# Second attention: when biases and weights to split are loaded, and where the probabilities are transposed

## The chip, the core and the metric

The kernel runs on one core of a Trainium2 chip. The metric is device time in microseconds (us), as the median of several executions. The core's engines are called PE (matrix products), ACT (scalar engine), DVE (vector engine), POOL (GpSimd) and SP, which here only issues DMA transfers. ACT issues some transfers too. All transfers of the core share 16 DMA engines.

## What is computed

One layer of an encoder, for two requests of 2048 tokens and width 1024, all in fp32:

```
proj = rms_norm(x) @ w_in
o_a  = windowed attention (8 query heads, 2 key heads)   * silu(g_a)
o_b  = neighbourhood attention (8 heads, 64-wide grid)   * silu(g_b)
x    = x + concat(o_a, o_b) @ w_out
y    = x + (p @ w_ple) * sigmoid(x @ w_ple_gate)
```

The neighbourhood attention lets a query of the 32 x 64 grid see 8 rows and 16 columns around it. Scores get a learned bias by relative place, and cells outside the window a bias of -1e30, so that softmax gives them zero:

```
sc = where(mask, einsum('bnqhd,banchd->bnhqac', qr, kb) * scale + bias, -inf)
pr = softmax(sc)
o  = einsum('bnhqac,banchd->bnqhd', pr, vb)
```

## The kernel before, in words

**Precision.** An fp32 product is made of three products of split operands: each operand is written as a high part in the type fp32r and a remainder, and high x high, high x low and low x high are added in PSUM. The split of an operand is a cast on ACT (high) and a subtraction on DVE or POOL (low). Weights that are used often are split once, in `presplit`: a block is loaded into the tile `pre` (L224), split, and stored to DRAM (`sp_...`, L217), from where the split parts are loaded later.

**Units.** The program runs 96 attention units, f = 0 to 95. Units 0 to 31 are the first attention, units 32 to 95 the second one: two halves of four heads, two requests, 16 blocks of 128 queries (4 blocks of rows by 4 of columns, the column block is cb = f mod 4). While the attention of unit f is on PE, the products of the input projection of a later unit (`pqk`, `pvg`: 48 matmuls of 512 columns) fill the room between its small products. A second attention's unit takes some 15 us. After the units comes the output projection.

**A unit of the second attention** (`unit_b`) does, for its four heads: scores on PE (`scb`) and a softmax step on DVE that adds the tile `bias` and takes the row maximum (L286); the exponentials on ACT (L310, tile `s`); transposes of the probabilities on PE (`pt`, tile `ptb`); their split by a cast on ACT and a subtraction on DVE (`p_t`, L946 and L947); the product with the values (`po`, tile `pob`, values in `vw`, loaded at L912); and the gate and the store (`fin`, store `ob_d` at L975).

**Copied and fp32 units.** PE transposes an fp32r tile faster than an fp32 one (medians of 227 and 272 ns a matmul). In most units (`copied_(f)`: 32 to 54 and 59 to 86) the exponentials are copied by DMA into the fp32r tile `tn` before they are transposed. ACT issues these four copies itself, right behind the exponentials:

```
if sink is None and turned is not None:
    waiting.append(i)
    for k in waiting[:1] if n_ in (1, 2) else waiting[:] if n_ == 3 else ():
        P(nc.scalar.dma_start(to.bitcast(F32), ss[k]))   # tn <- s, L319
```

The other units (55 to 58 and 87 to 95, the "fp32 units") transpose the fp32 tile directly (rows `ptb<-rowwise,s`).

**What sets the order.** Three things. A plan per kind of unit says at which share of the unit's PE work each step is put; `PLAN_C` is the one of the copied units, and an entry is (share, this unit or the one before, step, head). PE's order is pinned to it. The other engines' orders are made by a scheduler, which puts an instruction as early as its dependencies let it, unless it is wrapped in `P` (kept in the order in which the program was written) or has an added dependency (`after(load, ex)`: the load waits for that instruction by a semaphore). And a transfer takes one of eight completion counters (DMAHW0 to DMAHW7) in turn, over SP and ACT together; before it is issued, the transfer eight places before it, which had the same counter, has to be complete. An engine's queue is served in order, so whatever stands behind a waiting transfer on SP or ACT waits with it.

**The bias.** Two slots in turn hold the bias of a unit; a unit with cb = 2 uses the one of the unit before it. Its load (L897) must wait until the softmax steps that read the slot's old content are done. For a copied unit behind a copied unit the load also waits for the last exponential of the unit before (`last_ex[-1]`).

Of the kernel before, what the change touches and what calls it, by code (L numbers as in the profile page):

```python
# [11 lines left out]
F32 = mybir.dt.float32  # L12
# [7 lines left out]
NT = SEQ // 128  # L20
# [22 lines left out]
def row_type(b):  # L43
    return (0, 1, 1, 2)[b]


def col_type(cb):
    return (0, 1, 1, 2)[cb]
# [10 lines left out]
def bias_offsets():  # L59
# [44 lines left out]
PLAN_C = (  # L104
    (0.00, 1, "sc", 0), (0.03, 1, "sc", 1), (0.07, 1, "sc", 2), (0.09, 0, "po", 2), (0.11, 1, "sc", 3), (0.16, 0, "po", 3),
    (0.16, 1, "exp", 0), (0.24, 0, "fin", 0), (0.35, 1, "prep", 0),
    (0.60, 1, "pt", 0), (0.70, 1, "pt", 1), (0.80, 1, "pt", 2), (0.92, 1, "po", 0), (0.95, 1, "pt", 3), (0.98, 1, "po", 1),
)


def copied_(f):

    return 2 * NT <= f and not (4 * NT - 9 <= f < 4 * NT - 5 or f >= 6 * NT - 9)


def emit(ctx, tc, io):
    nc = tc.nc
# [56 lines left out]
    P = tc.keep_in_program_order  # L174
# [15 lines left out]
    def w_block(half, tag, j):  # L190

        if half == "p":
            return io["w_ple"][128 * j:128 * j + 128, 512 * tag:512 * tag + 512]
        if half == "o":
            h, c = int(tag[2]) - 1, int(tag[1]) - 1
            return io["w_out"][512 * h + 128 * j:512 * h + 128 * j + 128, 512 * c:512 * c + 512]
        c0 = 1280 + 1024 * half + (512 if tag == "wb" else 0)
        return io["w_in"][128 * j:128 * j + 128, c0:c0 + 512]
# [13 lines left out]
    def presplit(load):  # L212

        if load:
            if due:
                key, t, slot = due.pop()
                nc.sync.dma_start(parts_d[key], t[:, 0:2].bitcast(F32))  # L217
            if to_split and (to_split[0][0] in (0, 1) or combined):
                if not pre:
                    pre.extend([ap.tile([128, 4, 512], F32R, tag="raw", name="pre", bufs=1), 0])  # L220
                pre[1] += 1
                due.append((to_split.pop(0), pre[0], 2 + pre[1] % 2))
                key, t, slot = due[0]
                nc.sync.dma_start(t[:, slot].bitcast(F32), w_block(*key))  # L224
            else:
                pre.clear()
        elif due:
            key, t, slot = due[0]
            raw, sc = t[:, slot].bitcast(F32), nw[:, key[2]:key[2] + 1]
            if key[0] in ("p", "o"):  # L230
                behind(nc.scalar.copy(t[:, 0], raw))
                behind(nc.vector.tensor_tensor(out=t[:, 1], in0=raw, in1=t[:, 0].bitcast(F32), op=ALU.subtract))
            else:
                behind(nc.scalar.activation(t[:, 0], raw, AF.Copy, scale=sc))
                behind(nc.vector.scalar_tensor_tensor(out=t[:, 1], in0=raw, scalar=sc, in1=t[:, 0].bitcast(F32),
                                                      op0=ALU.mult, op1=ALU.subtract))
# [23 lines left out]
    def behind(ins, other=None):  # L260

        tc.add_manual_dep(ins.ins, (other or last_pe[-1]).name,
                          mybir.DependencyInfo(mybir.DependencyClass.NoSync, mybir.DependencyReason.DATA),
                          reason="behind the product")
# [25 lines left out]
    def sm_tiles():  # L290
        return {"s": [], **{k: ap.tile([128, 4], F32, tag=k, name=k, bufs=3) for k in ("mx", "nm", "den", "rd")}}

    last_ex = []

    def after(ins, other):

        tc.add_manual_dep(ins.ins, other.name, mybir.DependencyInfo(mybir.DependencyClass.Sync, mybir.DependencyReason.DATA),
                          reason="behind the copies")
# [111 lines left out]
    def big(shape, dt, name):  # L410
        return ap.tile(shape, dt, tag="big", name=name, bufs=3)
# [81 lines left out]
    for i in range(2):  # L493
        t = ap.tile([128, 2, 512], F32R, tag=f"q2{i}", name=f"q2{i}")
# [24 lines left out]
    def proj_a(f):  # L519
# [84 lines left out]
        for i, c in enumerate(project(pg, xr, lambda k, b: w_g[k][:, b, :], 215)):  # L604
            if i in HG and f > 0 and not early:
                split(f + 1, HG[i], low=nc.vector if f == 1 else nc.gpsimd)
            if i in HN and f > 0 and f not in last:
                square(f + 1, HN[i])
            if i == PR:
                queries()  # L610
            if i in (PA, PA + 16) and 1 < f < 2 * NT - 2:
                presplit(i == PA)
            if i == PA and f == 2 * NT - 2:
                store_last()
            if i == 7 and t == NT - 1:
                ps = ptile([128, 512], "ms", "pms")
                tr(ps[:NT, :128], ms_a[:, NT * s:NT * s + NT])
                row = ap.tile([128, 512], F32, tag="sq", name="row", bufs=2)
                P(nc.scalar.copy(row[:NT, :128], ps[:NT, :128]))
                P(nc.sync.dma_start(ms_d[s * SEQ:(s + 1) * SEQ].rearrange("(t p) -> t p", p=128), row[:NT, :128]))  # L620
            yield c
            if i + 24 == ka:
                keys_a(kt, t)
# [172 lines left out]
    def proj_b(f):  # L796
# [10 lines left out]
        for i, c in enumerate(project(pk, xr, lambda k, b: ready("wa", k, w_qk)[:, b, :], 215)):  # L807
            at = i + 24 if f in last else i
            if i == PD and f == 2 * NT + 9:
                stats_b(1)  # L810
            if at in HX:
                split(f + 1, HX[at])
            if i == PA and f >= 2 * NT + 2 and (to_split or due):
                presplit(True)
            yield c
# [18 lines left out]
        for i, c in enumerate(project(pv, xr, lambda k, b: ready("wb", k, w_vg)[:, b, :], 215)):  # L834
            if i + 24 in HX and f not in last:
                split(f + 1, HX[i + 24])
            if i == (PR if f not in last else 1):
                normed()
            if i == PA + 16:
                presplit(False)  # L840
            yield c
            if i == (KB if f not in last else 10):
                if f < 2 * NT + 2:
                    pending.append((kt, b, cb))
                else:
                    keys_b(kt, b, cb)
# [31 lines left out]
            nc.gpsimd.tensor_copy(q1[e][z:z + 64], q1[e][a:a + 64])  # L878
        return q1, q2

    bt = []

    def unit_b(f):
        half, st = divmod(f - 2 * NT, 2 * NT)
# [2 lines left out]
        _, gs = held[f]  # L887
# [4 lines left out]
        if cb != 2:  # L892
            off, _ = BIAS_OFF[(row_type(b), col_type(cb))]
            if not bt:
                bt.append(big([128, 2, 4, 512], F32, "bias"))
            bt.append(bt[0][:, len(bt) % 2])
            load = nc.sync.dma_start(bt[-1][:, :, :n],  # L897
                                     io["bias"][half][:, off:off + 4 * n].rearrange("p (h n) -> p h n", h=4))
            if f > 2 * NT and copied_(f) and copied_(f - 1):
                after(load, last_ex[-1])  # L900
        bias = bt[-1]
        vw = []

        def load_values():

            spare = f >= 6 * NT - 6 and f % 2 == 0
            if spare:
                four = ap.tile([128, 4, 4, 2 * HD], F32R, tag="raw", name="vw4", bufs=1)
            for j in range(nch):
                v = four[:, j] if spare else \  # L910
                    ap.tile([128, 4, 2 * HD], F32R, tag=("vp", "vr_")[j % 2], name="vw", bufs=3 - j % 2)
                load = nc.sync.dma_start(v[:kn[j]].bitcast(F32).rearrange("p h d -> p (h d)"),  # L912
                                         v_d[half, s, cb][r0 + ch[j][0]:r0 + sum(ch[j])]
                                         .rearrange("r c h a d -> (r c) (h a d)"))
                if copied_(f):
                    after(load, last_ex[2])
                vw.append(v)
# [4 lines left out]
        sm, p_ts, got = sm_tiles(), [], {}  # L922
# [45 lines left out]
        def fin(_):  # L968
            pgt = ptile([128, 2, 128], "sc", "pgtb")
            for i in range(2):  # L970
# [3 lines left out]
            nc.vector.tensor_tensor(out=o_t, in0=pgt, in1=o_t, op=ALU.mult)  # L974
            nc.sync.dma_start(ob_d[s][b, :, 2 * half:2 * half + 2, cb, :], o_t)  # L975
        return {"sc": sc, "pt": pt, "po": po, "fin": fin, "prep": lambda _: nxt(f),
                "exp": lambda _: (next(got["ex"]), load_values())}


    tiles = [(s, u) for s in range(2) for u in range(NU)]  # L980
# [89 lines left out]
    def nxt(f):  # L1070
        if f + 1 < 6 * NT:
            qs[f + 1] = prep_a(f + 1) if f + 1 < 2 * NT else prep_b(f + 1)
# [66 lines left out]
    for f in range(6 * NT):  # L1139
# [8 lines left out]
        for kv in range(2 if in_a else 1):  # L1148
            unit = unit_a(f, kv) if in_a else unit_b(f)
            for part, now, act, i in PLAN_A if in_a else PLAN_C if copied_(f) else PLAN_B:  # L1150
                at = (kv + part) / (2 if in_a else 1)
                while spent < at * total:
                    spent += next(stream, total)
                if now or prev:
                    (unit if now else prev)[act](i)
            prev = unit
# [323 lines left out]
```

## Time and profile before

| What | Value |
|---|---|
| median of 3 runs | 2468.09 us (2463.90, 2468.09, 2469.24) |
| profiled execution: its own time | 2468.76 us |
| profiled execution: span of the profile | 2466.9 us |
| mean granted PE clock | 0.999 of full speed |
| busy: PE / DVE / ACT / POOL | 99% / 69% / 57% / 35% |
| units 32 to 95 on PE | about 800 to 1820 us |
| units 55 to 58 on PE (transposes of `s`) | from 1175 us |
| bytes moved by DMA | 479.65 MB, mean 194 GB/s |

How to read the rows of the trace: a timeline row has the start in us, the duration, the engine, the line, the operation, output<-input, the shape, and in brackets the idle time of the engine just before it and what ended it. `SPq` and `ACTq` rows are issues of transfers, not the transfers. A row of a wait view has the waiting engine, line and what it waited for: us in total, number of times, longest. A row of the stage view has the stretch, its length, the busy time of each engine with its number of instructions, then the granted PE clock, the busy share of the DMA engines and the GB/s that they moved.

### The profile page before, as it was taken

Reading aid. Unit: us, or ns where it says so; the run is one execution under the profiler, and the core shown is the slowest. Engines: PE = TensorE matmul, PEld = TensorE weight load, DVE = VectorE, ACT = ScalarE, POOL = GpSimd, SP = SyncE. Lnnn points to the kernel's source line nnn. Section 1 sums busy time; section 2 is a strip of 40 time slices with the busy share of each in tenths; the row PEclk is TensorE's granted clock in tenths of the full one; section 3 lists DMA queues with packets and bytes.
Section 4 is the critical chain, followed back from the end, with each engine's and each line's share of the span. In section 5 each row is a group of like instructions: output and inputs, shape, how many; then the busy total and the mean of one; then the engine's idle time right before and its main releaser. Section 6 shows DMA issues by size and latency. Waiting matters only on the chain.

```text
span 2466.9 us, 40869 instructions
## 1 busy us (share of the span) xinstructions
PE 2443.6 (99%) x13062; PEld 2065.4 (84%) x13062; DVE 1702.1 (69%) x4214; ACT 1412.6 (57%) x3408; POOL 852.9 (35%) x1363
## 2 busy tenths in 40 slices
PE   9999999999999999999999999999999999999999
PEld 8888888888888888888888888878888888888887
DVE  7777777777765666666666666766537655677776
ACT  6777776777664665665666566665763212344443
POOL 4555555555543544554444444433110000000000
PEclk9999999999999999999999999999999999999999
DMA  6332223232254677767967687778977445856765
GB/s 227 122 103 93 95 88 103 95 101 90 93 180 140 212 243 237 234 211 252 305 222 228 207 266 254 246 241 265 312 237 272 156 166 176 269 178 210 247 226 171
DMA packets 275255, 479.65 MB, mean 194 GB/s; under 512 B 31168, under 2 KB 116064, under 8 KB 270816
## 3 DMA queue, kind: packets, MB, share of 16 engines
q1 hardware_dynamic: 245376, 437.84, 53.4%
q10 hardware_dynamic: 29664, 39.19, 5.2%
q8 instruction: 104, 1.70, 0.3%
q14 instruction: 111, 0.91, 0.1%
HBM read 307.72 MB, written 134.23 MB: 179 GB/s over the span
## 4 chain that ended last, share of the span: by engine, by line
PE 90%; DMA 4%; DVE 3%; ACT 2%; issue 1%; POOL 1%; SPq 0%; ACTq 0%; DVEq 0%; POOLq 0%
PE acca L1283 14%; PE pvg L267 14%; PE pqk L267 13%; PE accc L1283 11%; PE pq L267 6%; PE pg L267 6%; PE scb L267 4%; PE pob L267 3%; PE pk L267 3%; PE pple L267 3%; PE po L267 3%; PE sc L267 3%; PE pt L273 2%; DMA vw<-v_d 2%; PE ptb L271 2%; DMA tn<-s 1%
## 5 line engine op out<-in xcount | busy, mean ns | idle before, releaser
L267 PE MATMUL pvg<-wb,xr 128*128 128x512 f32 x1536 | 448.5, 404 | 0.0
L267 PE MATMUL pqk<-wa,xr 128*128 128x512 f32 x1536 | 444.1, 411 | 0.0
L310 ACT ACTIVATE s<-s,nm 128x320 f32<-128x320 f32 (+6 forms) x512 | 293.2, 574 | 150.4 <-DVE nm L307 118.9
L267 PEld LDWEIGHTS pvg<-wb,xr 128*128 128x128 f32 x1536 | 270.4, 189 | 33.5
L267 PEld LDWEIGHTS pqk<-wa,xr 128*128 128x128 f32 x1536 | 266.9, 189 | 37.5
L1265 ACT CAST opd<-raw 128x512 fp32r<-128x512 f32 x224 | 131.5, 619 | 270.3 <-PE acca L1283 118.0
L388 POOL TENSOR_TENSOR xr<-stx,xr 128x512 fp32r<-128x512 f32 x186 | 237.5, 1294 | 116.1 <-ACT xr L387 88.1
L1266 DVE TENSOR_TENSOR opd<-raw,opd 128x512 fp32r<-128x512 f32 x224 | 146.6, 686 | 146.6 <-ACT opd L1265 146.6
L267 PE MATMUL pg<-wb,xr 128*128 128x512 f32 x768 | 232.8, 409 | 1.0 <-DVE vv L545 1.0
L267 PE MATMUL pq<-wa,xr 128*128 128x512 f32 x768 | 219.4, 400 | 0.0
L947 DVE TENSOR_TENSOR p_t<-ptb,p_t 128x368 fp32r<-128x368 f32 (+5 forms) x256 | 120.6, 486 | 100.1 <-ACT p_t L946 97.9
L1283 PE MATMUL accc<-opd,wb 128*128 128x512 f32 x768 | 176.7, 389 | 0.0
L1283 PE MATMUL acca<-opd,wa 128*128 128x512 f32 (+1 forms) x780 | 175.9, 386 | 0.5 <-ACT r L1361 0.5
L1283 PE MATMUL acca<-opd,s 128*128 128x512 f32 x768 | 175.4, 389 | 0.0
L1283 PEld LDWEIGHTS acca<-opd,wa 128*128 128x128 f32 x780 | 144.9, 188 | 30.2 <-ACT r L1361 0.7
L1283 PEld LDWEIGHTS acca<-opd,s 128*128 128x128 f32 x768 | 144.1, 188 | 29.9
L1283 PEld LDWEIGHTS accc<-opd,wb 128*128 128x128 f32 x768 | 144.1, 188 | 29.9
L965 ACT COPY otb<-pob 64x512 f32<-64x512 f32 x128 | 74.4, 582 | 160.7 <-PE pob L267 158.9
L946 ACT CAST p_t<-ptb 128x368 fp32r<-128x368 f32 (+5 forms) x256 | 107.2, 425 | 101.7 <-PE ptb L271 59.8
L152 POOL TENSOR_TENSOR yb<-vrb,power 128x8 f32<-128x8 f32 x64 | 106.5, 1665 | 148.6 <-DVE vrb L822 124.2
L267 PEld LDWEIGHTS pob<-p_t,vw 128*128 128x128 f32 (+2 forms) x832 | 133.7, 189 | 28.2 <-DMA vw<-v_d 6.5
L267 PEld LDWEIGHTS pq<-wa,xr 128*128 128x128 f32 x768 | 135.1, 189 | 17.3
(173 smaller groups left out, 5191.5 us busy)
## 6 DMA issues: line engine op xcount, KB each, us to landing
stx<-x_b SPq DMA_DIRECT2D x128, 256.0 KB
vw<-v_d SPq DMA_DIRECT2D x96, 256.0 KB
stx<-x_a SPq DMA_DIRECT2D x64, 256.0 KB
stn<-x_n SPq DMA_DIRECT2D x64, 256.0 KB
v_d<-vb SPq DMA_DIRECT2D x64, 256.0 KB
ple_d<-ev SPq DMA_DIRECT2D x64, 256.0 KB
xres<-x_r SPq DMA_DIRECT2D x64, 256.0 KB
x_d<-r SPq DMA_DIRECT2D x64, 256.0 KB
```

Source lines behind the costliest of these rows:

```text
L152: nc.gpsimd.tensor_tensor(out=y, in0=v, in1=power.broadcast_to([128, n]), op=ALU.pow)
L267: pinned(nc.tensor.matmul(out, lhsT, rhs, start=start, stop=stop))
L271: pinned(nc.tensor.transpose(out.bitcast(F32R), in_, eye))
L273: pinned(nc.tensor.transpose(out, in_, eye.bitcast(F32)))
L310: ex = nc.scalar.activation(ss[i], ss[i], AF.Exp, bias=nm[:, i:i + 1], accum_out=den[:, i:i + 1])
L388: low.tensor_tensor(out=lo, in0=raw, in1=hi.bitcast(F32), op=ALU.subtract)
L946: nc.scalar.copy(hi, pf)
L947: nc.vector.tensor_tensor(out=lo, in0=pf, in1=hi.bitcast(F32), op=ALU.subtract)
L965: nc.scalar.copy(ot[a:a + 64], pq[z:z + 64])
L1265: P(nc.scalar.copy(hi, v))
L1266: P(nc.vector.tensor_tensor(out=lo, in0=v, in1=hi.bitcast(F32), op=ALU.subtract))
L1283: pinned(nc.tensor.matmul(ps[:, cols], w[k][:, a, c:c + 128], o[:, b, cols], start=i in (0, 1, 4) and k == 0 and j == 0, stop=k == 3 and j ...
```

## The change

Three edits; the arithmetic, the instructions and the bytes moved are the same.

```
 PLAN_C = (
     ... (0.16, 1, "exp", 0), (0.24, 0, "fin", 0), (0.35, 1, "prep", 0),
-    (0.60, 1, "pt", 0), (0.70, 1, "pt", 1), (0.80, 1, "pt", 2), (0.92, 1, "po", 0), (0.95, 1, "pt", 3), (0.98, 1, "po", 1),
+    (0.64, 1, "pt", 0), (0.73, 1, "pt", 1), (0.82, 1, "pt", 2), (0.93, 1, "po", 0), (0.96, 1, "pt", 3), (0.99, 1, "po", 1),
 )
@@ presplit
-                nc.sync.dma_start(t[:, slot].bitcast(F32), w_block(*key))
+                (P if key[0] in ("p", "o") else lambda ins: ins)(nc.sync.dma_start(t[:, slot].bitcast(F32), w_block(*key)))
@@ unit_b
-    bt = []
+    bt, ex_of = [], {}
...
-            if f > 2 * NT and copied_(f) and copied_(f - 1):
-                after(load, last_ex[-1])
+            k = f - (1 if copied_(f) else 3)
+            if copied_(k):
+                after(load, ex_of[k])
...
-                "exp": lambda _: (next(got["ex"]), load_values())}
+                "exp": lambda _: (next(got["ex"]), ex_of.update({f: last_ex[-1]}), load_values())}
```

The first edit moves the transposes of a copied unit later by 0.01 to 0.04 of the unit. The second keeps the 16 loads of `w_ple` and `w_out` blocks to be split in program order on SP. The third is the same as before for copied units; the bias load of an fp32 unit f now waits for the last exponential of unit f - 3, where that is a copied unit (f = 55, 56, 57, 87, 88, 89). Line numbers behind L899 grow by one.

**Place 1: SP in units 52 and 53, and ACT's copies there.** The 360-wide bias row with the DVE wait is that of fp32 unit 55, the 480-wide one that of unit 53 (`stx`: tokens of a later unit; names `v_d`: values of all units, in DRAM). Before:

```order
L370 DMA stx<-x_b 128x512 [waits DMAHW1_49,Pool_49]
L897 DMA bias<-bias 128x4x360 [waits DMAHW2_49,DVE_49]
L975 DMA ob_d_86<-o_tb 128x2x128 [waits DMAHW4_49,DVE_49]
L912 DMA vw<-v_d_302 120x512 [waits DMAHW6_49,PE_49,Activation_49]
L912 DMA vw<-v_d_302 120x512 [waits DMAHW7_49]
L912 DMA vw<-v_d_302 120x512 [waits DMAHW3_49,DMAHW1_49,PE_49]
L897 DMA bias<-bias 128x4x480 [waits DMAHW3_49,Activation_49]
```

After, from unit 53's bias on:

```order
L897 DMA bias<-bias 128x4x480 [waits DMAHW2_49,Activation_49]
L855 DMA v_d_303<-vb 8x8x512 [waits DMAHW3_49,DVE_49]
L855 DMA v_d_304<-vb 16x8x512 [waits DMAHW4_49]
L855 DMA v_d_305<-vb 8x8x512 [waits DMAHW5_49]
L370 DMA stx<-x_b 128x512 [waits DMAHW6_49,Pool_49]
L370 DMA stx<-x_b 128x512 [waits DMAHW7_49,DMAHW1_49,Pool_49]
L897 DMA bias<-bias 128x4x360 [waits DMAHW0_49]
L976 DMA ob_d_86<-o_tb 128x2x128 [waits DMAHW2_49,DVE_49]
```

Unit 55's bias stood in unit 52's stretch of the queue, ahead of unit 53's own; now it stands in unit 53's stretch, and no longer waits for DVE. The copies on ACT, unit 52 before (360 wide):

```order
L319 DMA tn<-s 128x360 [waits DMAHW3_49,DMAHW2_49,Activation_49]
L310 ACTIVATE s,den<-s,nm 128x360
L319 DMA tn<-s 128x360 [waits DMAHW5_49,Activation_49]
L310 ACTIVATE s,den<-s,nm 128x360 [waits DMAHW6_49]
L319 DMA tn<-s 128x360 [waits DMAHW0_49,Activation_49]
L319 DMA tn<-s 128x360 [waits DMAHW2_49,Activation_49]
L875 ACTIVATE q1b<-pqtb,wk 64x256 [waits PE_49]
```

and unit 53 after (480 wide):

```order
L319 DMA tn<-s 128x480 [waits DMAHW3_49,Activation_49]
L310 ACTIVATE s,den<-s,nm 128x480 [waits DMAHW7_49]
L319 DMA tn<-s 128x480 [waits DMAHW6_49,Activation_49]
L319 DMA tn<-s 128x480 [waits DMAHW0_49,Activation_49]
L875 ACTIVATE q1b<-pqtb,wk 64x256 [waits PE_49]
```

In unit 52 the fourth copy had the counter DMAHW2 behind unit 55's bias; now that fourth copy follows an `stx` load, and it is the fourth copy of unit 53 that has the counter of unit 55's bias, DMAHW0. Units 84 and 85, with unit 87's bias, stand to each other in the same way.

**Place 2: SP in units 69 and 70.** `pre<-w_ple` is a block to split. Before:

```order
L655 DMA sums_237<-raw 128x2048
L370 DMA stx<-x_b 128x512 x2
L224 DMA pre<-w_ple 128x512 x2
L975 DMA ob_d_85<-o_tb 128x2x128
L912 DMA vw<-v_d_307 128x512 x2
L912 DMA vw<-v_d_307 96x512
L912 DMA vw<-v_d_307 128x512
L855 DMA v_d_308<-vb 8x8x512
L855 DMA v_d_309<-vb 16x8x512
L370 DMA stx<-x_b 128x512 x2
```

After:

```order
L655 DMA sums_237<-raw 128x2048
L370 DMA stx<-x_b 128x512 x2
L976 DMA ob_d_85<-o_tb 128x2x128
L913 DMA vw<-v_d_307 128x512 x2
L913 DMA vw<-v_d_307 96x512
L913 DMA vw<-v_d_307 128x512
L855 DMA v_d_308<-vb 8x8x512
L855 DMA v_d_309<-vb 16x8x512
L224 DMA pre<-w_ple 128x512
L370 DMA stx<-x_b 128x512 x2
```

The pair of loads in unit 69 is gone; one stands in unit 70, ahead of the two `stx` loads, and from there on each of these loads stands ahead of `stx` instead of behind it.

**Place 3: PE, the transposes of a copied unit**, as one piece of the difference:

```order
 L267 MATMUL pqk<-wa_9495,xr 128x512 x3
-L267 MATMUL pqk<-wa_9497,xr 128x512 x2
+L267 MATMUL pqk<-wa_9497,xr 128x512 x3
+L267 MATMUL pqk<-wa_9499,xr 128x512
 L271 MATMUL ptb<-rowwise,tn 96x128 x3
-L267 MATMUL pqk<-wa_9497,xr 128x512
-L267 MATMUL pqk<-wa_9499,xr 128x512 x3
-L267 MATMUL pqk<-wa_9501,xr 128x512
+L267 MATMUL pqk<-wa_9499,xr 128x512 x2
+L267 MATMUL pqk<-wa_9501,xr 128x512 x3
 L271 MATMUL ptb<-rowwise,tn 96x128 x3
```

The first two heads' transposes stand two of the 24 `pqk` matmuls later; the third and fourth, further down, one later; the `pob` products keep their places.

## The prediction

> **What bounds the kernel now.** I read the page's first part, then who waited for whom on PE.
>
> ```profile
> span 2466.9 us, 40869 instructions
> PE 2443.6 (99%) x13062; PEld 2065.4 (84%) x13062; DVE 1702.1 (69%) x4214; ACT 1412.6 (57%) x3408; POOL 852.9 (35%) x1363
> ...
> PE ptb L271 <- DMA tn<-s: 6.8, 4, 2.9
> PE pob L267 <- DMA vw<-v_d: 3.3, 8, 1.1
> PE scb L267 <- DVE mx L286: 2.1, 1, 2.1
> ```
>
> PE is the bound, and the change leaves its instructions alone. So it can win only PE's idle time, 2466.9 - 2443.6 = 23.3 us in all, or what that idle time does to the clock. The largest item is transposes that wait for copied probabilities: 6.8 us, and only four times. The timelines of PE, ACT and of the issues on SP and ACT show where (in each group: bias or weights issued, the unit's first copy issued, the end of ACT's wait, PE's).
>
> ```profile
> 1119.17 0.38 SPq L897 DMA_DIRECT2D bias<-bias  x1
> 1120.68 0.47 ACTq L319 DMA_DIRECT2D tn<-s  x1
> 1126.63 0.47 ACT L875 ACTIVATE q1b<-pqtb,wk 64x256 fp32r<-64x256 f32 x1 [4.09 <-DMA bias<-bias]
> 1126.78 0.44 PE L271 MATMUL ptb<-rowwise,tn 128*120 128x128 f32 x3 [1.87 <-DMA tn<-s]
> ...
> 1394.72 0.81 SPq L224 DMA_DIRECT2D pre<-w_ple  x2
> 1399.65 0.47 ACT L875 ACTIVATE q1b<-pqtb,wk 64x256 fp32r<-64x256 f32 x1 [2.43 <-DMA pre<-w_ple]
> 1401.23 0.53 PE L271 MATMUL ptb<-rowwise,tn 128*128 128x128 f32 x4 [1.91 <-DMA tn<-s]
> ...
> 1636.49 0.38 SPq L897 DMA_DIRECT2D bias<-bias  x1
> 1638.00 0.47 ACTq L319 DMA_DIRECT2D tn<-s  x1
> 1644.76 0.47 ACT L875 ACTIVATE q1b<-pqtb,wk 64x256 fp32r<-64x256 f32 x1 [4.90 <-DMA bias<-bias]
> 1645.10 0.56 PE L271 MATMUL ptb<-rowwise,tn 128*120 128x128 f32 x3 [2.88 <-DMA tn<-s]
> ```
>
> These are units 52, 69 and 84, the three in which a large load that belongs to a later unit is issued 1.5 us or less ahead of the copies (1120.68 - 1119.17 = 1.51; 1638.00 - 1636.49 = 1.51). Two things follow. The copies share the DMA engines with that load and land late, so the first transposes wait. And ACT, whose fourth copy has the load's completion counter, is held until the load is complete. All three loads are the ones that the change moves.
>
> The stretches around the stalls show a second price, in the clock (the column before the last two):
>
> ```profile
> 1125.00:1130.00 5.00, 3.22 (x20) 2.68 (x21) 2.71 (x5) 3.32 (x9) 1.62 (x3) 1.00 0.96 255
> 1400.00:1405.00 5.00, 3.77 (x17) 3.20 (x18) 4.05 (x8) 3.13 (x8) 0.79 (x2) 0.79 0.98 315
> 1405.00:1410.00 5.00, 5.00 (x30) 4.26 (x29) 1.18 (x3) 2.68 (x6) 2.54 (x2) 0.87 0.13 36
> 1645.00:1650.00 5.00, 4.90 (x20) 3.97 (x21) 4.21 (x9) 4.45 (x11) 1.45 (x3) 0.66 0.82 256
> ```
>
> Behind two of the three stalls the granted clock falls: 5 x (0.21 + 0.13) = 1.70 us lost behind 1401, 5 x 0.34 = 1.70 behind 1645, none behind 1126. What it cost PE is seen from a unit's first transpose to its last product, against an undisturbed unit of the same shape:
>
> ```profile
> 1409.07 0.57 PE L267 MATMUL pob<-p_t,vw 128*128 128x256 f32 x4
> 1662.72 0.45 PE L271 MATMUL ptb<-rowwise,tn 128*128 128x128 f32 x4
> 1669.02 0.57 PE L267 MATMUL pob<-p_t,vw 128*128 128x256 f32 x4
> 1132.82 0.47 PE L267 MATMUL pob<-p_t,vw 120*128 120x256 f32 x3
> 1652.52 0.47 PE L267 MATMUL pob<-p_t,vw 120*128 120x256 f32 x3
> ```
>
> Unit 69: 1409.07 - 1401.23 = 7.84 us, against 1669.02 - 1662.72 = 6.30: 1.54 more. Unit 84: 1652.52 - 1645.10 = 7.42, against 1132.82 - 1126.78 = 6.04: 1.38 more. So the dips cost 2.9 us (3.4 by the clock column).
>
> **The bias loads (third edit).** For copied units the wait is the old one. Unit 55's and unit 87's loads leave the stretches of units 52 and 84 and go one unit on, behind the `stx` loads there:
>
> ```profile
> 1131.84 1.60 SPq L370 DMA_DIRECT2D stx<-x_b  x2
> 1139.07 0.47 ACTq L319 DMA_DIRECT2D tn<-s  x1
> ...
> 1650.77 1.83 SPq L370 DMA_DIRECT2D stx<-x_b  x2
> 1658.77 0.47 ACTq L319 DMA_DIRECT2D tn<-s  x1
> ...
> 1135.00:1140.00 5.00, 5.00 (x29) 4.19 (x27) 4.00 (x12) 2.33 (x6) 2.40 (x2) 1.00 0.11 40
> 1655.00:1660.00 5.00, 5.00 (x29) 4.17 (x28) 3.87 (x11) 2.63 (x7) 2.24 (x2) 1.00 0.05 21
> ```
>
> The exponential of three units back is long done by then, so the new wait itself holds nothing; its effect is the place. The load is issued at about 1133.4 and 1652.6 on the old time scale, 5.6 and 6.2 us ahead of the unit's first copy instead of 1.5, thus over 4 us more lead. With the old landing time the stall would be at most 2.88 - 4.1, below nothing. The bytes fit too: behind those places the DMA engines stood at 0.11 and 0.05 of 5 us, and 720 KB at the 256 GB/s of the row at 1645 are 2.8 us. ACT's fourth copy there has the bias's counter. It is issued some 2 us behind the first, so 7.7 and 8.2 us behind the load. In units 52 and 84 ACT was free again at 1126.6 and 1644.8, 7.5 and 8.3 us behind the load, so ACT may wait a few tenths. PE does not see that: `q1b` serves the next unit. Bounds: both stalls fully gone, -4.75; or both reappear in units 53 and 85, 0. I take -4.75. Queued behind the load on SP is `ob_d`, which waits for DVE some 5.8 us anyway (295.3 / 51 in the row below).
>
> **The loads to split (second edit).** The pair of unit 69 goes, so 512 KB leave the place ahead of its copies. Its late issue has a row too (the second; the first is that of `ob_d`):
>
> ```profile
> SPq L975 <- DVE o_tb L974: 295.3, 51, 8.5
> ...
> SPq L224 <- DMA sums<-raw: 4.9, 1, 4.9
> ```
>
> SP stood 4.9 us in front of the pair for the completion of `sums`. That counter now belongs to the unit's third copy, which comes behind 1394.72, when `sums` was complete. From unit 70 on each load (256 KB, about 1 us at 256 GB/s) stands ahead of two `stx` loads instead of behind them. `stx` feeds a split a unit later, so 1 us more is covered; without that cover it would be 1 us in 15 units. The splits of `pre` stay at their places on ACT and DVE, 40 projection matmuls behind the load's place. Bounds: -1.91 or 0; I take -1.91.
>
> **The transposes (first edit).** The first two heads' transposes come two matmuls later:
>
> ```profile
> 1127.05 1.40 PE L267 MATMUL pqk<-wa,xr 128*128 128x512 f32 x5
> 1128.29 0.36 PE L271 MATMUL ptb<-rowwise,tn 128*120 128x128 f32 x3
> ```
>
> Five `pqk` matmuls take 1.24 us, two 0.5 us: so much more time for the copies. That covers the fourth and smallest stall, unit 86's 0.17 us (6.83 is the sum of the four), whose bias is not moved. The matmuls only change places, so the move itself costs PE nothing. What comes nearer is the last head's transpose to the next unit's third score product, which takes over its PSUM bank (three banks in turn):
>
> ```profile
> 1132.96 0.46 DVE L947 TENSOR_TENSOR p_t<-ptb,p_t 120x288 fp32r<-120x288 f32 x1 [1.21 <-ACT p_t L946]
> 1134.97 0.39 PE L267 MATMUL scb<-ks_b,q1b 128*128 128x480 f32 x1
> ```
>
> DVE is done with the bank at 1133.42, the product comes at 1134.97: 1.55 us of room, of which one matmul takes 0.25. No cost. The `pob` products keep their places and the `vw` loads theirs, so I leave the 3.3 us there (bounds: none, or twice as much).
>
> **Sum.** 1.87 + 2.88 + 1.91 + 0.17 = 6.83 us of stalls and 2.9 us of dips make 9.7. The profiled execution took 2468.76 us, so 2459.0; the median, 2468.09, is 0.67 below it, so **2458.4 us**. Behind the stalls PE is bound everywhere, so what is won there reaches the end.
>
> The Trainium skill, TensorE: Matmul & The Clock Gate, Part 1 and its closing table, says that the clock falls to half after an idle window of some 3.4 us, and to avoid PE gaps over about 3 us. The size agrees (1.70 us is half of 3.4); the cause does not: rows 1401 and 1645 dip behind 1.91 and 2.88 us. By the Trainium skill these gaps would be harmless to the clock; what would then follow is rival 1.
>
> **Rivals.**
> 1. The dips are not owed to these stalls (the gap of 1.87 us has none, and one of 2.1 us in the list above stays) and come elsewhere, or the median's executions had fewer of them: only 6.8 us are won, 2461.3. For it: one stall in three without a dip. Against: in the stage view of the whole span in steps of 20 us only the two stretches with these two stalls are below 1.00.
> 2. The stalls move with the loads: units 53 and 85 wait for the bias, a unit behind 69 for its weights. Unit 86 has this very order now:
>
> ```profile
> 1673.98 0.38 SPq L897 DMA_DIRECT2D bias<-bias  x1
> 1675.59 0.47 ACTq L319 DMA_DIRECT2D tn<-s  x1
> 1679.88 0.53 PE L271 MATMUL ptb<-rowwise,tn 128*128 128x128 f32 x4 [0.17 <-DMA tn<-s]
> ```
>
> There even 1.6 us of lead cost only 0.17. If two of three stalls came back, 2 to 3 us with their clock would be won: 2465.5.
> 3. Slower: the bank of the last transpose. If DVE reaches it 1.3 us later than now, the third score product waits in every copied unit, 51 of them. From that point on each 0.2 us costs 51 x 0.2 = 10 us: 2458.4 + 20 = 2478 at 0.4. Against it: 1.3 us is three of DVE's steps of that kind, and DVE waited 1.21 us for work just ahead.
>
> **How the numbers follow.** Forecast 0.60, rival 1 0.20, rival 2 0.14, rival 3 0.06. A run of three rounds can tell about 0.2% from no change, 4.9 us, so below 2463.2 is faster. That gives faster 0.80 (forecast and rival 1), same 0.14, slower 0.06. The forecast's own range is 2456.0 (some `vw` waits go with the loads) to 2460.5. The range reaches over rival 1 and most of rival 2: 2455.5 to 2465.5.
>
> **What would show it.** Right: no PE wait of `ptb` for `tn` over 0.5 us; no ACT wait for `bias` in units 52 and 84 nor for `pre` in 69; clock 1.00 in all stretches from 800 to 1820; PE busy unchanged but for the dips, and some 13 us idle left. Wrong: waits of `ptb` in units 53, 85 or 70 to 72, or a new wait of `scb` for DVE in many units. The forecast falls if the dips remain without the stalls.

## The result, and the profile after

The changed kernel took 2463.16 us (median of 20 executions, 2458.59 to 2466.03), the kernel before beside it 2468.16 us (median of 20, 2463.14 to 2473.02). The ratio is 0.9983, with a 95% interval of 0.9976 to 0.9990. So the change wins 5.0 us by the medians and 4.3 by the means; 9.7 were forecast. The gain is surely there. Against the line that the prediction drew for "faster" it can't be placed: by the medians (2463.16 against 2463.2) it lies just past that line, by the ratio (0.17% against 0.2%) just short of it.

The page of the changed kernel, the span and the row of busy times:

```profile
span 2459.8 us, 40879 instructions
PE 2442.1 (99%) x13062; PEld 2065.0 (84%) x13062; DVE 1701.3 (69%) x4214; ACT 1407.7 (57%) x3408; POOL 850.7 (35%) x1363
```

The view of who waited for whom, its two largest rows on PE and the one of the bias on ACT (us in total, times, longest):

```profile
PE scb L267 <- DVE mx L286: 3.2, 1, 3.2
PE pob L267 <- DMA vw<-v_d: 3.0, 6, 0.6
...
ACT q1b L875 <- DMA bias<-bias: 1.7, 1, 1.7
```

and the row of the kernel before that answers to the last one:

```profile
ACT q1b L875 <- DMA bias<-bias: 11.3, 3, 4.9
```

PE's idle time is 2459.8 - 2442.1 = 17.7 us, against 23.3. No row `ptb <- DMA tn` is left: all four stalls of 6.8 us are gone. ACT's 11.3 us behind `bias` are down to 1.7 us, one wait, in unit 86, whose load was not moved; ACT's row for `pre` is gone too. The profiled execution took 2461.64 us, 7.1 less than that of before. But the stall of the score product in unit 92, 2.11 us before, is 3.16 now, and the clock dips behind it. The timelines of ACT, DVE and PE there, in the changed kernel:

```profile
1757.76 0.58 ACT L1062 COPY ev<-pple 128x512 f32<-128x512 f32 x1 [4.06 <-DMA ple_d<-ev]
1759.02 0.69 DVE L1001 TENSOR_TENSOR p_r<-p,p_r 128x512 fp32r<-128x512 f32 x1 [4.60 <-ACT p_r L1000]
1760.14 0.61 PE L267 MATMUL scb<-ks_b,q1b 128*128 128x288 f32 x1 [3.16 <-DVE mx L286]
```

and its stages (length, PE's busy time and instructions, granted clock, DMA share, GB/s):

```profile
1735.00:1740.00 5.00, 5.00 (x33) 1.00 1.05 357
1740.00:1745.00 5.00, 5.00 (x30) 1.00 1.06 398
1745.00:1750.00 5.00, 5.00 (x31) 1.00 1.06 402
...
1755.00:1760.00 5.00, 1.98 (x12) 0.91 0.99 377
1760.00:1765.00 5.00, 4.86 (x15) 0.50 0.69 184
1765.00:1770.00 5.00, 5.00 (x29) 0.91 0.96 304
```

From 1735 on the DMA engines are full. A store of the per-layer path (`ple_d<-ev`) completes late, and ACT is held for 4.06 us at the next evacuation into that buffer. The cast of `p_r` behind it comes late. DVE, whose next step is the subtraction that goes with this cast, stands idle for 4.60 us, does its softmax step only behind that, and PE waits 3.16 us for it. The clock loses 5 x (0.09 + 0.50 + 0.09) = 3.4 us. In the profile of before the same place had 2.11 us and no dip. That is the first candidate for the missing half.

The second candidate is the profile of before itself: the sum was made from one execution.

### The profile page after: what moved, and what is told of

Same layout as the page of the kernel before. It is cut to its first block, busy times and chain, and to the rows that moved or that the text cites. A ratio compares the mean times of both kernels' runs of the same rounds, so it can differ in the third digit from the quotient of the medians.

```text
span 2459.8 us, 40879 instructions
## 1 busy us (share of the span) xinstructions
PE 2442.1 (99%) x13062; PEld 2065.0 (84%) x13062; DVE 1701.3 (69%) x4214; ACT 1407.7 (57%) x3408; POOL 850.7 (35%) x1363
## 4 chain that ended last, share of the span: by engine, by line
PE 91%; DMA 4%; DVE 3%; ACT 1%; POOL 1%; issue 1%; SPq 0%; ACTq 0%; DVEq 0%
PE pvg L267 14%; PE acca L1284 14%; PE pqk L267 13%; PE accc L1284 11%; PE pq L267 6%; PE pg L267 6%; PE scb L267 4%; PE pk L267 3%; PE pob L267 3%; PE po L267 3%; DMA vw<-v_d 3%; PE pple L267 3%; PE sc L267 3%; PE pt L273 2%; PE ptb L271 2%; DVE pr L750 1%
```

## The experiments

Two theories for the half that did not come. **Given back**: the three stalls were as large as priced, but the changed kernel loses more at unit 92. **One execution**: the stalls and dips differ from execution to execution, and the one profiled showed more than a usual one. First come the single edits, then attempts to take unit 92's stall away, then the two kernels profiled again. In the expectations from the pinned pair on, theory A is "one execution" and theory B "given back". Those of the single edits have another question too: whether the places of the loads made the stalls ("place"), or whether it is the later transposes that removed them ("transposes").

**The bias loads alone** (third edit):

```
...
-            if f > 2 * NT and copied_(f) and copied_(f - 1):
-                after(load, last_ex[-1])
+            k = f - (1 if copied_(f) else 3)
+            if copied_(k):
+                after(load, ex_of[k])
...
```

> The kernel before with the third edit alone: the bias load of an fp32 unit waits for the exponential three units back; weights and transposes stay as before. Theory (place): the stalls of units 52 and 84 go (1.87 and 2.88 us) with the clock dip behind the second, the one of unit 69 (1.91 us) stays with its dip; about 1 to 3 us are given back at the 2.1 us stall of unit 92, where the scores wait for DVE, because that stall grew to 3.16 us with a dip in the changed kernel. Net 2.5 to 5 us less than before, 2463 to 2466. Rival (transposes): the later transposes are what removed the stalls; then both stalls stay here, less at most some tenths, and the time is that of before, 2467 to 2469.

Measured: 2464.24 us (12 executions) against 2467.64 (35), ratio 0.9984, interval 0.9975 to 0.9994. The timeline of PE:

```profile
1398.91 0.53 PE L271 MATMUL ptb<-rowwise,tn 128*128 128x128 f32 x4 [0.94 <-DMA tn<-s]
1672.78 0.53 PE L271 MATMUL ptb<-rowwise,tn 128*128 128x128 f32 x4 [1.08 <-DMA tn<-s]
1763.68 0.61 PE L267 MATMUL scb<-ks_b,q1b 128*128 128x288 f32 x1 [3.45 <-DVE mx L286]
```

The stalls of units 52 and 84 are gone and come up nowhere else. Unit 69, which this edit does not touch, has 0.94 instead of 1.91; unit 86 has 1.08 instead of 0.17. Those two were the first sign that the sizes are not fixed.

**The loads to split alone** (second edit):

```
-                nc.sync.dma_start(t[:, slot].bitcast(F32), w_block(*key))
+                (P if key[0] in ("p", "o") else lambda ins: ins)(nc.sync.dma_start(t[:, slot].bitcast(F32), w_block(*key)))
```

> The kernel before with the second edit alone: the 16 loads of blocks to split keep their place on SP. Theory (place): only the stall of unit 69 goes (1.91 us, in the profile before with a dip of 1.5 us); units 52 and 84 still wait 1.87 and 2.88 us. Net 1.5 to 3.4 us less, less what unit 92 gives back (up to 1): 2465 to 2467.5. Rival (transposes): nothing changes, 2467 to 2469.

Measured: 2465.63 us (12), ratio 0.9990, interval 0.9979 to 1.0000. The timeline of PE:

```profile
1125.85 0.44 PE L271 MATMUL ptb<-rowwise,tn 128*120 128x128 f32 x3 [1.68 <-DMA tn<-s]
1641.05 0.44 PE L271 MATMUL ptb<-rowwise,tn 128*120 128x128 f32 x3 [2.17 <-DMA tn<-s]
1765.90 0.40 PE L267 MATMUL scb<-ks_b,q1b 128*128 128x288 f32 x1 [4.03 <-DVE mx L286]
```

Unit 69's stall is gone, units 52 and 84 keep theirs, and no clock dip stands behind either of them: the granted clock is 1.00 in all stretches of 20 us from 800 to 1760.

**The transposes alone** (first edit):

```
-    (0.60, 1, "pt", 0), (0.70, 1, "pt", 1), (0.80, 1, "pt", 2), (0.92, 1, "po", 0), (0.95, 1, "pt", 3), (0.98, 1, "po", 1),
+    (0.64, 1, "pt", 0), (0.73, 1, "pt", 1), (0.82, 1, "pt", 2), (0.93, 1, "po", 0), (0.96, 1, "pt", 3), (0.99, 1, "po", 1),
```

> The kernel before with the first edit alone: transposes of the copied units 0.01 to 0.04 of a unit later. Theory (place): the loads still stand ahead of the copies, so the three stalls stay and each is shorter by the two matmuls, 0.5 us: about 1.4, 1.4 and 2.4 us, the 0.17 us of unit 86 gone; 1.5 to 1.7 us less, and the dips may or may not follow: 2465 to 2468. Rival (transposes): the three stalls are gone and the time is that of the changed kernel, 2463. A cost of the later transposes, if there is one, would show as a wait of the score products for DVE in many units.

Measured: 2465.73 us (12), ratio 0.9992, interval 0.9983 to 1.0001. Its waits on PE:

```profile
PE ptb L271 <- DMA tn<-s: 2.9, 5, 1.3
PE scb L267 <- DVE mx L286: 1.7, 1, 1.7
```

The stalls stay in units 52, 69 and 84, all smaller than in the first profile, together 2.9 us. The score products wait for DVE once, in unit 92, as before: the last transpose's PSUM bank costs nothing. So the places of the loads made the stalls; the later transposes only shorten them.

The single edits give 3.4, 2.0 and 1.9 us by the medians, 7.3 together, where all three at once give 5.0 (by the means 9.1 and 4.3). The intervals of the second and the third edit reach 1.0000 and 1.0001, so alone each of these is at the edge of what the runs can tell. The gains overlap, since the first edit shortens the same waits that the other two take away; how much of the difference is this and how much is chance is not shown.

Unit 92 has a clock dip behind its stall in each of these three profiles (stalls of 3.45, 4.03 and 1.7 us; the largest dip stage of each, in the order above):

```profile
1765.00:1770.00 5.00, 5.00 (x17) 0.52 0.83 228
1765.00:1770.00 5.00, 4.10 (x14) 0.66 0.70 204
1765.00:1770.00 5.00, 5.00 (x20) 0.68 0.76 179
```

Of the five profiles of the kernel before that follow below, one has a dip there. That speaks for something being given back.

**The per-layer path paced**: the changed kernel with one weight load a chunk instead of two or one, so that fewer transfers meet the stores ahead of unit 92.

```
-            if m % 4 == 3 and (n < 3 or m == 3):
+            if m == 3:
                 load_coming()
```

> The changed kernel with one more edit: of the 8 blocks of output weights that are loaded while the position products run beside the last units, one instead of two per group of eight products is loaded in the first three groups; the others come three groups later. This takes up to 1.5 MB out of the stretch around 1740 to 1760 us, in which the DMA engines are busy throughout and ACT waits 2.9 and 4.1 us for a store to free its buffer, which ends as PE's 3.16 us stall in unit 92. Theory (given back in unit 92): the stall shrinks to under 1 us and its dip (about 3 us in the profile after) goes, the time falls by 2 to 5 us to 2458 to 2461, unless the loads now make waits in the groups behind the units (1820 to 1880 us, DMA busy share 0.92 to 0.99). Rival (the missing part is clock dips spread anywhere, not unit 92): the stall goes but the time stays within 1.5 us of 2463.

Measured: 2461.26 us (12), ratio to the kernel before 0.9974, interval 0.9964 to 0.9985, which overlaps that of the changed kernel. In the profile, of the slowest of the 12 executions (2468.14 us), unit 92 still stalls:

```profile
PE scb L267 <- DVE mx L286: 3.1, 1, 3.1
```

So pacing does not take that stall away in every execution; whether it does in the faster ones is not shown. The scheduler puts the loads as early as it can, and they bunch again in the queue of SP: seven `wb` loads are issued between 1717 and 1755, in the changed kernel eight. The next pair pins them.

**The same with the loads kept in their place**, on the kernel before (without the three edits) and on the changed kernel:

```
-            nc.sync.dma_start(w.bitcast(F32), parts_d[key])
+            P(nc.sync.dma_start(w.bitcast(F32), parts_d[key]))
...
-            if m % 4 == 3 and (n < 3 or m == 3):
+            if m == 3:
```

> The kernel before with two lines of the per-layer path changed, and none of the three edits: the weight loads keep the place in SyncE's order at which they are written, and one is written after every fourth piece of a chunk. This takes the bunch of transfers away that made the store ple_d late at unit 92. Theory A: unit 92's stall goes (2 to 4 us with its dip), the three others stay: 2464 to 2466. Theory B: in the kernel before that stall cost 2.1 us and no dip, so 2465.5 to 2466.5. Against both: the stores are late for another reason, unit 92 stalls by 2 us or more as before, and the time is that of the kernel before within 0.5 us.

> The changed kernel with the same two lines. Its distance to the kernel before with these lines is what the three edits win where unit 92 gives nothing back. Theory B: 7 us or more below that one, 2457 to 2459. Theory A: 4 to 6 us below it, as without the two lines, 2459 to 2461. If the loads now come late instead: waits of TensorE on the weights wb in the per-layer stages, and no gain.

Measured, beside a kernel before of 2466.52 us (19 executions): without the edits 2463.24 (12), ratio 0.9987, interval 0.9978 to 0.9996; with them **2457.91** (8), ratio 0.9967, interval 0.9954 to 0.9979. This is the fastest of all kernels here. Its page gives a span of 2456.2 us. Its three largest waits on PE (the second and the third are as before):

```profile
PE pob L267 <- DMA vw<-v_d: 3.7, 9, 0.8
PE pwarm L267 <- DVE warm L414: 1.5, 1, 1.5
PE pg L267 <- DVE vv L545: 1.0, 1, 1.0
```

and three of its stages, the same stretches as above:

```profile
1740.00:1745.00 5.00, 5.00 (x30) 1.00 0.90 318
...
1755.00:1760.00 5.00, 5.00 (x30) 1.00 0.63 215
1760.00:1765.00 5.00, 5.00 (x30) 1.00 0.85 227
```

Unit 92's stall is gone with its dip; the DMA share there is 0.90 and 0.63 where it was 1.06 and 0.99. Between 1717 and 1755 two `wb` loads are issued. ACT's hold at that evacuation is 0.28 us here, and 0.86 in the pinned kernel without the edits, where PE does not stall either. In all twelve profiles here in which PE stalls, its stall is ACT's wait at that evacuation less 0.9 us: 3.01 and 2.11 us in the profile of before, 4.06 and 3.16 after, 5.04 and 4.14 in the longest. So the chain read above (late store, ACT, DVE, PE) is what made that stall.

Now the test: with unit 92's stall away on both sides, the three edits win 2463.24 - 2457.91 = 5.3 us by the medians and 4.9 by the means (4.28 with the stall there; the 95% intervals of the means, worked out by resampling the executions, are 3.0 to 7.0 and 2.8 to 5.8). Had all of the missing 4.7 us been given back at unit 92, it would be near 9.7. That is excluded. The difference of the two wins is 0.6 us, resampled in the same way -1.8 to 3.1, so a give-back of up to some 3 us is not excluded. Theory "given back" does not carry the whole miss. (The distance of the two pinned kernels is the one that theory A expected; the time of 2457.91 itself lies in theory B's band, since the pinned kernel without the edits came out below both expectations.)

The profile of the pinned kernel without the edits shows the other end. It is of its slowest execution (2470.79 us, where the median is 2463.24). Its waits of the transposes, and three of its stages:

```profile
PE ptb L271 <- DMA tn<-s: 8.8, 4, 2.6
```

```profile
1125.00:1130.00 5.00, 3.71 (x14) 0.66 0.98 265
...
1400.00:1405.00 5.00, 3.00 (x12) 0.76 0.98 345
...
1680.00:1685.00 5.00, 3.63 (x16) 0.75 0.89 271
```

The stalls there add up to 8.8 us, with dips behind three of them, one behind 1126, where the first profile had none.

**The two kernels once more**, unchanged, four executions of before and two of after:

> The kernel before once more, unchanged, for a second profiled execution. Theory A (the profiled execution that the sum was made from showed more than a usual one: the three stalls and the clock dips behind two of them are partly chance): the same three stalls at units 52, 69 and 84, but 4 to 6 us together instead of 6.66, and at most one of them with a dip behind it; TensorE's idle time some 1 to 2 us under 23.3. Theory B (that execution was usual, and the changed kernel gave half of the gain back at unit 92): 6.5 to 7 us of stalls again, dips behind 1401 and 1645 again, and unit 92 at about 2.1 us without a dip.

> The kernel before, unchanged, a third profiled execution. Theory A (the landing of the bias and weight loads differs from one execution to the next, so the three stalls are partly chance): over this and the next two executions the four waits of the last transposition for its copies add up to anything between 1 and 9 us, on average 4 to 6, with none to three clock dips behind them; ScalarE's wait for the bias in units 52 and 84 is 4 us or more in some and missing in others. Theory B (the second profile was the exception and the sum of 6.83 us is usual): 6 to 9 us in all three, ScalarE held by the bias in both units each time.

> The kernel before, unchanged, a fourth profiled execution; expected as for the third: theory A 1 to 9 us and different from it by 2 us or more, theory B 6 to 9 us.

> The kernel before, unchanged, a fifth profiled execution; expected as for the third. If A holds, executions with small waits are also the fast ones: a time near 2463 with waits of 1 to 3 us, near 2470 with 7 us or more and dips.

> The changed kernel once more, unchanged. Theory A: unit 92's stall is anywhere between 1.5 and 4 us, as in the single edits, and the dip behind it comes and goes. Theory B: unit 92's stall is 3 us or more again with granted clocks of 0.5 to 0.9 behind it between 1755 and 1770, since the change itself made that stall grow. Both: no wait of the last transposition on a load in units 52, 69 and 84.

> The changed kernel, unchanged, a third profiled execution. Both theories: no wait of the last transposition for its copies over 0.5 us in units 52, 69, 84 and 86. Unit 92 again between 2 and 4 us. A clock dip, where there is one, stands behind unit 92 or behind a wait for the weights vw, not at 1401 or 1645.

Measured, PE's waits on the copies unit by unit from its timelines, and the clock lost behind them from the stages of 5 us (1 minus the granted clock, times the length):

| execution of before | its time, us | unit 52 | 69 | 84 | 86 | sum | clock lost there | unit 92 (clock lost) |
|---|---|---|---|---|---|---|---|---|
| the one of the prediction | 2468.76 | 1.87 | 1.91 | 2.88 | 0.17 | 6.83 | 3.4 | 2.11 (0) |
| second | 2463.08 | 0.20 | 0.71 | 0 | 0 | 0.91 | 0 | 2.28 (1.7) |
| third | 2465.28 | 1.00 | 1.79 | 1.99 | 1.20 | 5.98 | 0 | 2.51 (0) |
| fourth | 2467.29 | 0.72 | 1.85 | 1.77 | 1.37 | 5.71 | 1.7 | 2.48 (0) |
| fifth | 2464.25 | 1.01 | 1.32 | 0.34 | 1.88 | 4.55 | 1.7 | 1.85 (0) |
| mean | 2465.73 | 0.96 | 1.52 | 1.40 | 0.92 | 4.8 | 1.4 | 2.2 (0.3) |

The rows of the waits view that carry the sums, of the second, third, fourth and fifth:

```profile
PE ptb L271 <- DMA tn<-s: 0.9, 3, 0.4
```

```profile
PE ptb L271 <- DMA tn<-s: 6.0, 4, 2.0
```

```profile
PE ptb L271 <- DMA tn<-s: 5.7, 4, 1.9
```

```profile
PE ptb L271 <- DMA tn<-s: 4.5, 5, 1.9
```

Theory "one execution" stands in this: 0.9 to 6.8 us for the same program, and the first profile is the largest of five in both columns. (The second, with 0.9, lies below what either theory expected of it.) But the five together are not usual either. Their mean time, 2465.73 us, is 1.8 under the mean of the 20 executions at the top (2467.50). Some of that may be the session, as the kernel before took 2466.5 us beside the second and 2466.25 beside the third to fifth. But the fastest of the five has the smallest stalls and the slowest the largest, so a usual execution may hold more than the 4.8 and 1.4 us of the last row.

Why the executions differ is seen in unit 52 of the second one (issues on SP and ACT, and ACT's next step):

```profile
1119.55 0.38 SPq L897 DMA_DIRECT2D bias<-bias  x1
1121.43 0.47 ACTq L319 DMA_DIRECT2D tn<-s  x1
1123.93 0.47 ACTq L319 DMA_DIRECT2D tn<-s  x1
1124.45 0.47 ACT L875 ACTIVATE q1b<-pqtb,wk 64x256 fp32r<-64x256 f32 x1 [1.15 <-PE pktb L273]
```

The bias is issued 1.88 us ahead of the first copy, hardly more than the 1.51 of the prediction's row, and the fourth copy, which needs the load's counter, goes out at 1123.93: the load was complete 4.4 us after its issue or sooner. In the first profile that copy went out 6.9 us after the load's issue, and ACT's next step came at 1126.6. Unit 84 shows it without any difference in the lead, which is 1.5 us in all five executions. Its load and its fourth copy in the second execution, where PE does not wait at all:

```profile
1634.00 0.38 SPq L897 DMA_DIRECT2D bias<-bias  x1
1638.42 0.47 ACTq L319 DMA_DIRECT2D tn<-s  x1
```

From the first execution to the fifth this distance is 7.75, 4.42, 7.04, 7.01 and 5.55 us, and PE's stall 2.88, 0, 1.99, 1.77 and 0.34 us: the later the load is complete, the longer PE waits, without an exception. The order of the instructions is the same. What decides when the load lands was not tried.

The changed kernel's two further executions took 2466.78 and 2461.80 us. Neither has a wait of `ptb` for `tn`. Unit 92 on PE's timeline and the stage behind it, of the first:

```profile
1765.11 0.61 PE L267 MATMUL scb<-ks_b,q1b 128*128 128x288 f32 x1 [4.14 <-DVE mx L286]
```

```profile
1765.00:1770.00 5.00, 4.89 (x15) 0.50 0.66 174
```

and of the second, with another wait that has a dip behind it:

```profile
1675.47 0.37 PE L267 MATMUL pob<-p_t,vw 96*128 96x224 f32 x1 [0.96 <-DMA vw<-v_d]
1761.33 0.40 PE L267 MATMUL scb<-ks_b,q1b 128*128 128x288 f32 x1 [2.24 <-DVE mx L286]
```

```profile
1675.00:1680.00 5.00, 4.14 (x18) 0.75 0.55 170
...
1760.00:1765.00 5.00, 3.67 (x15) 0.78 0.76 246
```

Over its three executions unit 92 costs 3.2 us and 2.8 us of clock on average, against 2.2 and 0.3 over the five of before. That speaks for a give-back of about 3.4 us; the pinned pair, with more executions, speaks for 0.6 (4.9 - 4.28). The profiled executions agree among themselves: 4.8 + 1.4 - 3.4 leaves 2.8 us, and their mean times differ by 2465.73 - 2463.41 = 2.3. The 4.3 us between the means of 20 are more, which fits if the five of before hold less than usual. How much is given back, between nothing and some 3 us, stays open, and also why that stall is larger behind the change.

## Why the prediction was right, and where its size was wrong

**What bounds, and what can be won.** Right. PE's busy time hardly moved (2443.6 to 2442.1), and all that was won was idle time and clock. The sign "some 13 us idle left" was worked out wrong: it takes the 2.9 us of dips out of the idle time, but they lie in PE's busy time. Without them it is 23.3 - 6.8 = 16.5 us, and 17.7 were measured.

**The bias loads.** Right in place. Units 52 and 84 have no wait, units 53 and 85 got none, in all three profiles of the changed kernel; the few tenths on ACT did not come up. The size was off: -4.75 was priced for the pair, 0.96 + 1.40 = 2.4 us is the mean over five executions, with dips that come and go. Alone, the edit measured 3.4 us.

**The loads to split.** Right: unit 69's stall went and none came up behind it. 1.91 was priced, 1.52 is the mean, 2.0 us was measured for the edit alone.

**The transposes.** The step was right that they cost nothing and cover unit 86. It was priced too low: 0.17 us was that execution's value, 0.92 the mean. The same row stood as evidence against rival 2 ("even 1.6 us of lead cost only 0.17"); in three other executions that order cost 1.20, 1.37 and 1.88 us. The argument was not sound, though rival 2 did not happen.

**The dips.** 2.9 us was the second term of the sum. The dips do stand behind these stalls in some executions, but none, one or two of them: 1.4 us by the clock column on average, where 3.4 stood in the first. And the sign "clock 1.00 in all stretches from 800 to 1820" failed: all three profiles of the changed kernel have a dip behind unit 92, two of them another at 1130 or 1675 behind a wait for `vw`. The condition "the forecast falls if the dips remain without the stalls" is met in part.

**The step that failed** is the sum, "6.83 us of stalls and 2.9 us of dips make 9.7", in the size of its terms. Both were sized from one execution; over five they are 4.8 and 1.4, 6.2 us in all, which would account for 3.5 of the missing 4.7 us. This share may be too large, since the five of before may hold less than usual. And the sum lacked a term for unit 92: the forecast left the 2.1 us there alone, and did not ask whether that wait would stay as it was. By the profiles this term is about 3.4 us, by the pinned pair 0.6. Which of the two carries more of the miss stays open. The forecast's base did not help to see it, since the first execution's total lay only 0.67 us above the median of three: a total near the median does not make its parts usual.

**The range.** The measured 2463.16 lies outside the forecast's own range, 2456.0 to 2460.5. It lies inside the wide one, 2455.5 to 2465.5, only because that takes in rival 1 and most of rival 2. So the places and the direction were foreseen, and the size was not.

**The rivals.** Rival 1 (2461.3) comes nearest to 2463.16, and its second half says a part of why: "the median's executions had fewer of them". It spoke of the dips alone; the stalls themselves were smaller too. Rival 2's time (2465.5) is 2.3 us off, but its mechanism is not seen. Rival 3 (2478) is refuted: no score product waits for a bank in the 51 copied units.

The clock rule that the prediction weighed (the Trainium skill, TensorE: Matmul & The Clock Gate, Part 1: half clock after an idle window of some 3.4 us) does not agree with the runs in its threshold: dips stand behind 0.96, 1.77 and 1.88 us, and none behind 2.48 and 2.51. In one thing the same part agrees: it says that the window runs freely and the ramp differs from run to run, and here the same stall has a dip in one execution and none in the next. No run here shows whether a free window is the reason.

## What to carry to other kernels

A stall that is read from one profiled execution is a draw, not a price: where a transfer's landing decides it, look at a second and third execution of the same program before it is summed, price by the mean, and compare the times of these executions with the usual one: here the fastest had the smallest stalls and the slowest the largest. A wait on which nothing is done is not a constant either: unit 92's cost more behind the change, and a stretch in which the DMA engines are full is a place to expect that. And loads that a scheduler may hoist may have to be pinned before a change of their place shows: in the one profile of the paced kernel the stall of unit 92 was still 3.1 us, with the loads pinned and paced it was gone, for 2457.91 us in all.

## What the runs showed of the hardware

The same 720 KB load, issued at the same place of the same program, was complete in 4.4 us or less in one execution; in others the copy that needs it complete went out only 7.0 to 7.75 us after its issue. The size of an idle gap of PE does not by itself decide whether the granted clock dips: behind 2.51 us there was none, behind 0.96 us (and 0.39 soon after) there was one, with the same loss, 5 x 0.25 + 5 x 0.09 = 1.7 us, as behind gaps of two to three times that length (the second stage is 1680 to 1685 of that execution):

```profile
1680.00:1685.00 5.00, 5.00 (x28) 0.91 0.10 20
```

A loss of twice that, 3.4 us, stood behind gaps of 3.16, 3.45 and 4.14 us, but also in the paced kernel at 1160 to 1175, behind waits for `vw` of 1.27 and 0.47 us, and behind one gap of 4.03 us it was 1.7.

Whether these stalls make the scatter of a kernel's time is not shown. The kernel before spread by 2.8 us (standard deviation of 20 executions), the changed one by 2.0, the fastest one by 1.9 (8). But the paced kernel, in whose profile no transpose waits for its copies, spread by 3.1 (12), and the one with the first edit alone, which has such waits, by 1.4 (12).
